# Wider warm-up products, earlier residual loads and one more raw weight tile in a single-core encoder layer

## The chip, the cores and the metric

The kernel runs on one core of a Trainium2 chip. The metric is the time in device microseconds of one execution. Each core has a matrix engine (TensorE, PE in the profile; its weight loads are PEld), a vector engine (VectorE, DVE), a scalar engine (ScalarE, ACT), a general engine (GpSimd, POOL) and a queue engine (SyncE, SP). DMAs are issued by SP, by POOL and, at the very end, by ACT.

## The reference

One layer of an encoder for 512 prompt tokens and 64 later tokens, in float32, with a model width of 1024, and a final norm:

```
x = x + Mixer(RMSNorm(x))          # gated DeltaNet branch and GLA branch, gated merge, then w_o
x = x + CrossAttn(RMSNorm(x), mem) # 4 heads into 256 memory tokens (w_mk, w_mv, w_mq, w_mo)
x = x + ConvFFN(RMSNorm(x))        # w_up, causal conv of width 3, SiLU gate, w_down
y = RMSNorm(x)
```

The recurrent states, the convolution tails and the memory keys and values are outputs too. The residual x has to be added back three times: after w_o, after w_mo and after w_down.

## The kernel before, in words

Activations lie feature-major: x is eight tiles of 128 features by 576 tokens (`x[0]` to `x[7]`). A weight tile is 128 partitions by 1024 columns, 512 KB. Every product is made in three passes of a reduced-precision float32 type: each operand is split into a high part and a low remainder, and high times high, low times high and high times low are summed in PSUM. For most weights the low part is not subtracted on an engine: ACT writes the negated high part, and a DMA that POOL issues adds the original weights onto it (`split_summed`, "accumulate" below). In the profile such a DMA is `w<-wt` or, where its source is a sum of weight blocks that lies in SBUF, `w<-ws`. The output projection w_o (`wo`), half of the gates, w_mo and most of the FFN use a scheme with seven block products per pair of tiles (`products`, named P1, Q5, Q6, P2, P3, Q7, Q4).

No scheduler of the framework orders the work. The kernel has its own planner, `Driver`: it goes through the program in PE's order, keeps a modelled clock `now`, estimates a start for every vector, scalar, POOL and DMA instruction from the costs in `FIXED` and `PACE`, and emits all of them in the order of these starts. Each engine then runs its own list in order and waits on semaphores. Small differences of modelled time can so swap neighbours in an engine's list, or move an operation that may run on DVE or on POOL (`X`) from one to the other.

Raw weights come by SP into the tiles `raw` (`RAWB` of them, in the pool `wp`, and after the mixer one more, `rawf`); in the profile that load is `wr<-wt`. A raw tile is free again when its split is done. Split weights lie in nine `w` tiles at that stage.

At the start PE multiplies a tile of ones with itself (`warm`, `NWARM` times) while the first x tiles and weights load and are split. Then come the q and k tiles of head 0 (`first2`, 16 groups of six products over 256 and 320 columns). Much later, `ATT` sets the order `mk 0, mv 0, mk 1, mk 2, wo, mv 1, mq 0, ...`: memory keys, the first memory values, more keys, the output projection w_o, and so on. Ahead of `wo` the eight residual tiles are loaded again from `xT` in pairs by `x_again`, since their first copies were given up: the pair 0 and 1 at the first memory values, and each next pair when w_o's product P1 for the pair before has been planned (`wo_finish`). The software descriptors of POOL's DMAs lie in a scratch at the foot of SBUF, with its default size.

Of the kernel before, what the change touches and what calls it, by code (L numbers as in the profile page):

```python
# [17 lines left out]
P = 128  # L18
# [7 lines left out]
SLOT = 584  # L26
HT = T // 2
NS = 56
RAWB = 3
WB = 6  # L30
WF = 3
RF = 1
# [2 lines left out]
HOP = 0.2  # L35
BACK = 6.0
MARGIN = 0.6
NWARM = 20


C_GMIX, C_GKV, C_GMEM, C_GFFN, C_GFIN = 0, 8, 16, 24, 32
# [417 lines left out]
def tile_trunk(ctx, tc, xT, memT, wt, wd, vec, cst, w0, wgate, st_gdn, st_conv, st_gla, st_ffn, ckT, cv,  # L459
               o_y, o_gdn_p, o_conv, o_gla_p, o_ffn, o_mk, o_mv, o_gdn_s, o_gla_s):  # L460
    nc = tc.nc
# [18 lines left out]
    def nm(s):  # L480
        cnt[0] += 1
        return f"{s}{cnt[0]}"
# [48 lines left out]
    def f(ap):  # L531
        return ap.bitcast(F32)
# [5 lines left out]
    def keep(t_):  # L538
        drv.pending.add(t_[:].tensor.name)
        return t_  # L540
# [5 lines left out]
    def raw_tile():  # L546
        if fp is not None and drv.first("rawf", RF, "raw", RAWB):
            return keep(drv.rotate("rawf", RF, fp.tile([P, 1024], F32, tag="rawf", name=nm("wr"), bufs=RF)))
        return keep(drv.rotate("raw", RAWB, wp.tile([P, 1024], F32, tag="raw", name=nm("wr"), bufs=RAWB)))

# [123 lines left out]
    ones_r = cp.tile([P, 128], F32R, name="onesr")  # L674
# [4 lines left out]
    G.memset(mhalf, -0.5)  # L679
    pw = pq.tile([P, 512], F32, tag="sm", name=nm("warm"))  # L680
    for _ in range(NWARM):
        PE.matmul(pw[:, 0:128], ones_r, ones_r, start=True, stop=True)


    vec_t = cp.tile([P, NV], F32, name="vec")
# [4 lines left out]
    x = []  # L690
    raws = [wp.tile([P, 1024], F32, tag="raw", name=nm("wr"), bufs=RAWB) for _ in range(2)]
    for t_ in raws:
        keep(drv.rotate("raw", RAWB, t_))

# [151 lines left out]
    def xs_of(hl, w=T):  # L846
        return [(a[:, 0:w], b[:, 0:w]) for a, b in hl]
# [697 lines left out]
    def products(pairs, ops, finish, late=None):  # L1545

        banks = {}
        for pair, prod in product_order(pairs, late is not None):
            if prod == "Q5" and late is not None:
                yield late  # L1550
                late = ()
            bank = pair, "b" if prod in ("Q5", "P3") else "c" if prod == "P2" else "a"
            start = bank not in banks
            if start:
                banks[bank] = sm()
            a, b, c = (banks[pair, i][:, 0:HT] if (pair, i) in banks else None for i in "abc")
            o = banks[bank][:, 0:HT]
            wh, wl = weight("*", (pair, prod), False)
            n = len(ops)
            for i, op in enumerate(ops):  # L1560
                h, lo = op[prod]
                PE.matmul(o, wh[:, 128 * i:128 * i + 128], h, start=start and i == 0, stop=False, skip_group_check=True)
                PE.matmul(o, wh[:, 128 * i:128 * i + 128], lo, start=False, stop=False, skip_group_check=True)
                yield 0.4
            for i, op in enumerate(ops):
                PE.matmul(o, wl[:, 128 * i:128 * i + 128], op[prod][0], start=False, stop=i == n - 1, skip_group_check=True)
            finish(pair, prod, a, b, c)
            drop(wh)
            fetch(wpos[0])
            yield 0.4  # L1570
# [8 lines left out]
    def xslot(i, s="x"):  # L1579

        return drv.rotate(f"F{i}", 1, fp.tile([P, SLOT], F32R if s != "x" else F32, tag=f"F{i}", name=nm(s), bufs=1))


    def main():
# [51 lines left out]
        for k in range(KT + 1):  # L1636
            for i, ps in enumerate(first2):
                j = k - i
# [164 lines left out]
        def x_again(m):  # L1803

            for i in (m, m + 1):
                x[i] = xslot(i)
                DMA(x[i][:, 0:T], xT[:, i, :])
# [6 lines left out]
        def wo_finish(pair, prod, a, b, c):  # L1814
            m = pair[0][1]
            xx, scale = (x[m], 0.5) if prod in ("P1", "Q6", "P3", "P2") else (x[m + 1], -0.5)
            half = N1 if prod in ("P1", "P2", "Q4") else N2
            V.scalar_tensor_tensor(xx[:, half], b if prod in ("Q5", "P3") else c if prod == "P2" else a, scale, xx[:, half],
                                   op0=ALU.mult, op1=ALU.add)
            if prod == "P1" and m < 6:  # L1820
                x_again(m + 2)
            if prod == ("P2" if m == 6 else "P3"):
                drv.spawn(c_norm(m, C_GMEM, acc, out))
            elif prod == "Q4":
                drv.spawn(c_norm(m + 1, C_GMEM, acc, out))

        def c_norm(m, gcol, acc_, out_):
            yield [x[m]]
            sq_acc(acc_, x[m], m == 0)
            drv.done.add(("sq", m))  # L1830
            if drv.ready(*(("sq", i) for i in range(8))):
                drv.spawn(c_rstat("n2", [(acc_, 0)], 4, True, 2.0))
            while not drv.ready("wo"):
                yield WAIT
            out_.append((m, norm_prep(x[m], vcol(gcol + m))))
            drv.done.add(("norm", gcol, m))

        for kd, i in ATT:
            if kd == "mk":
                yield from mem_keys(i)  # L1840
            elif kd == "mv":
                if i == 0:
                    x_again(0)
                yield from mem_values(i)
            elif kd == "wo":
                yield tuple(("wops", m) for m in range(1, 8, 2))
                yield from products(WPAIRS, [wops[m] for m in range(1, 8, 2)], wo_finish)
                drv.done.add("wo")
            else:
                if i == 0:  # L1850
                    yield tuple(("norm", C_GMEM, m) for m in range(8))
                    xs = xs_of([p for _, p in sorted(out, key=lambda t: t[0])])
                ckr, cvr = slot("ckr"), slot("cvr")
                DMA(r4(ckr[:, 0:512], 256), ckT[:, 2 * i:2 * i + 2, :])
                DMA(r4(cvr[:, 0:512], 256), cv[:, 256 * i:256 * i + 256].rearrange("(a p) d -> p a d", p=P))
                N["ks", i], N["vs", i] = split(ckr), cvr
                for m in (2 * i, 2 * i + 1):
                    b = []
                    yield from tile_proj("mq", m, xs, b)
                    if m == 0:  # L1860
                        yield ("n2",)
                        use_norm("n2")
                    q = slot("q")
                    evac(b[0], two(q))
                    h, lo = slot("qh", F32R), slot("ql", F32R)
                    A.copy(h[:, 0:T], q[:, 0:T])
                    X.tensor_tensor(lo[:, 0:T], q[:, 0:T], f(h[:, 0:T]), op=ALU.subtract)
                    N["q", m] = (h, lo)
                drv.spawn(c_att(i))
# [230 lines left out]
        for kd, i in FFN[:-1]:  # L2100
            if kd == "up":
                j = i
# [24 lines left out]
            elif kd == "dn1":  # L2127
                m, p = i
# [113 lines left out]
    def mem_keys(hd):  # L2242

        kr = slot("kraw")
        for j in range(2):
            wh, wl = weight("mk", 2 * hd + j)
            ps = big()
            for k in range(KT):
                a, b = N["mx"][k]
                mm3([(ps[:, 0, 0:256], slice(0, 256))], wh, wl, a, b, k, k == 0, k == 7)  # L2250
                if k % 2:
                    yield 0.7
            V.tensor_tensor(kr[:, 256 * j:256 * j + 256], ps[:, 0, 0:256], N["mbc"][:, 0:256], op=ALU.mult)
        DMO(o_mk[256 * hd:256 * hd + 256, :].rearrange("(j p) t -> p j t", p=P), r4(kr[:, 0:512], 256))
        N["k", hd] = split(kr)

    def mem_values(nh):

        vr = [slot("vraw") for _ in range(2)]
        ps = big()  # L2260
        for kp in range(4):
            wh, wl = weight("mv", nh * 4 + kp)
            for tt in range(2):
                c = slice(128 * tt, 128 * tt + 128)
                for k in range(2):
                    a, b = N["mx"][2 * kp + k]
                    w1, w2 = wh[:, 512 * k:512 * k + 512], wl[:, 512 * k:512 * k + 512]
                    PE.matmul(ps[:, tt, :], a[:, c], w1, start=(kp == 0 and k == 0), stop=False)
                    PE.matmul(ps[:, tt, :], a[:, c], w2, start=False, stop=False)
                    PE.matmul(ps[:, tt, :], b[:, c], w1, start=False, stop=(kp == 3 and k == 1))  # L2270
                    yield 1.0
        for tt in range(2):
            for j in range(2):
                A.activation(vr[j][:, 256 * tt:256 * tt + 256], ps[:, tt, 256 * j:256 * j + 256],
                             AF.Identity, scale=N["mrt"][:, tt:tt + 1])
        for j in range(2):
            hd = 2 * nh + j
            DMO(o_mv[:, 256 * hd:256 * hd + 256].rearrange("(a p) d -> p a d", p=P), r4(vr[j][:, 0:512], 256))
            N["v", hd] = split(vr[j])
# [153 lines left out]
```

## Time and profile before

| | |
|---|---|
| median of 3 runs | 1107.15 us (1104.71 to 1108.14) |
| the profiled execution | 1107.82 us, span 1106.1 us |
| PE busy | 1087.6 us (98% of the span) |
| DVE, ACT, POOL busy | 746.8, 700.5, 313.6 us |
| mean granted TensorE clock | 0.996 |
| DMA moved | 173.04 MB, mean 156 GB/s |
| DMAs that POOL issues | 209: 147 `w<-wt`, 33 `w<-wd` (w_down), 29 `w<-ws` |

Times inside the span are counted from its start. A row of the timeline has a start, a duration (from the start of the first to the end of the last where it is a group), the engine, the source line, the operation and its count; in brackets stands how long the engine had been idle, and what ended that. Nearly all rows say L257, the line of the planner's helper that records every operation, so they are told apart by tile names. Matmuls overlap in the rows, since each one's duration includes its way through the array; the distance between starts is the pace. PEclk in a table of windows is the clock granted to TensorE, 1.00 being full.

### The profile page before, as it was taken

How to read it: one execution, taken by the hardware profiler on the slowest of the kernel's cores; microseconds unless marked ns; L12 is line 12 of the kernel's file. 1: busy time of each engine (PE TensorE's matmuls, PEld its weight loads, DVE VectorE, ACT ScalarE, POOL GpSimd, SP SyncE). 2: the span in 40 equal slices, each digit the busy share in tenths (PEclk: the TensorE clock that was granted, in tenths of full speed). 3: DMA queues.
4: the chain of work that ended last, by engine and by line, in shares of the span. 5: the costliest groups of instructions: out<-in, count | busy, mean ns of one | idle time of the engine just before them, and what ended most of it. 6: DMA issues, size and time to landing. Idle time of an engine off the chain costs nothing. (4 is left out here: it accounts for less than half of the span.)

```text
span 1106.1 us, 21400 instructions
## 1 busy us (share of the span) xinstructions
PE 1087.6 (98%) x8215; PEld 1049.5 (95%) x8215; DVE 746.8 (68%) x1466; ACT 700.5 (63%) x1383; POOL 313.6 (28%) x539
## 2 busy tenths in 40 slices
PE   9999999999999999999999999999999999999997
PEld 8999989998988999998899999999999999999997
DVE  5566854864655866886746668768877777577766
ACT  6665645563755568465746658767776776668645
POOL 1243315230422232022110123334342333334222
PEclk9999999999999999999999999999999999999999
DMA  8666532453455778698792718766887888789754
GB/s 283 136 157 147 119 77 77 83 121 96 116 121 126 182 160 206 203 248 204 187 260 52 180 37 200 186 140 138 186 180 166 184 187 180 152 203 192 166 100 120
DMA packets 66886, 173.04 MB, mean 156 GB/s; under 512 B 7776, under 2 KB 14048, under 8 KB 66784
## 3 DMA queue, kind: packets, MB, share of 16 engines
q0 software_dynamic: 30096, 72.89, 38.4%
q1 hardware_dynamic: 36400, 98.26, 27.8%
q8 instruction: 65, 1.06, 0.4%
q10 hardware_dynamic: 288, 0.52, 0.1%
q14 instruction: 37, 0.30, 0.1%
HBM read 158.67 MB, written 5.37 MB: 148 GB/s over the span
## 5 line engine op out<-in xcount | busy, mean ns | idle before, releaser
L257 PE MATMUL big<-xh,w 128*128 128x256 f32 (+2 forms) x1568 | 293.0, 304 | 1.6 <-ACT xh L257 1.0
L257 POOL DMA_DIRECT2D w<-wt x147 | 131.0, 905 | 393.7 <-ACT w L257 265.7
L257 PEld LDWEIGHTS big<-xh,w 128*128 128x128 f32 x1568 | 235.9, 190 | 6.9 <-issue 2.0
L257 ACT CAST w<-wr 128x512 fp32r<-128x512 f32 (+3 forms) x201 | 158.6, 791 | 24.6 <-PE big L257 9.6
L257 PE MATMUL big<-xl,w 128*128 128x256 f32 (+2 forms) x784 | 168.4, 296 | 0.3 <-DVE xl L257 0.3
L257 ACT ACTIVATE w<-wr 128x512 fp32r<-128x512 f32 (+3 forms) x180 | 142.6, 793 | 38.1 <-PE sm L257 15.8
L257 PE MATMUL sm<-xh,w 128*128 128x290 f32 (+1 forms) x768 | 162.0, 298 | 0.6 <-ACT fu L257 0.5
L257 PE MATMUL sm<-ach,w 128*128 128x288 f32 (+2 forms) x624 | 128.8, 299 | 6.2 <-DMA w<-ws 2.6
L257 PEld LDWEIGHTS big<-xl,w 128*128 128x128 f32 x784 | 131.7, 189 | 0.7 <-DVE xl L257 0.7
L257 PEld LDWEIGHTS sm<-xh,w 128*128 128x128 f32 x768 | 126.3, 189 | 1.1 <-ACT fu L257 1.1
L257 PE MATMUL big<-ach,w 128*128 128x256 f32 x624 | 111.4, 295 | 0.5 <-ACT ach L257 0.5
L257 PEld LDWEIGHTS sm<-ach,w 128*128 128x128 f32 x624 | 102.0, 190 | 8.0 <-DMA w<-ws 3.1
L257 PE MATMUL sm<-xl,w 128*128 128x290 f32 (+1 forms) x384 | 103.1, 297 | 0.0
L257 PEld LDWEIGHTS big<-ach,w 128*128 128x128 f32 x624 | 94.6, 188 | 0.8 <-ACT ach L257 0.7
L257 ACT CAST w<-ws 128x512 fp32r<-128x512 f32 (+1 forms) x124 | 73.1, 602 | 31.1 <-DVE ws L257 15.3
L257 PE MATMUL sm<-acl,w 128*128 128x288 f32 (+2 forms) x312 | 84.7, 297 | 0.0
L257 DVE SCALAR_TENSOR_TENSOR fc<-fu,vec,fc 128x578 f32<-128x578 f32 x88 | 71.3, 828 | 7.6 <-ACT fc L257 7.2
L257 PEld LDWEIGHTS sm<-xl,w 128*128 128x128 f32 x384 | 71.8, 190 | 0.0
L257 DVE TENSOR_TENSOR w<-ws,w 128x512 fp32r<-128x512 f32 (+1 forms) x93 | 61.5, 673 | 14.3 <-ACT w L257 13.1
L257 PE MATMUL big<-acl,w 128*128 128x256 f32 (+1 forms) x312 | 66.7, 295 | 0.3 <-DVE acl L257 0.3
L257 PE MATMUL sm<-sh,w 128*128 128x290 f32 x288 | 61.5, 297 | 0.0
L257 PEld LDWEIGHTS sm<-acl,w 128*128 128x128 f32 x312 | 59.0, 191 | 0.0
(397 smaller groups left out, 2204.9 us busy)
## 6 DMA issues: line engine op xcount, KB each, us to landing
wr<-wt SPq DMA_DIRECT2D x134, 512.0 KB, 5.8
w<-wt POOLq DMA_DIRECT2D x60, 512.0 KB, 7.0
w<-wt POOLq DMA_DIRECT2D x87, 256.0 KB, 5.8
wr<-wd SPq DMA_DIRECT2D x24, 384.0 KB, 6.2
w<-wd POOLq DMA_DIRECT2D x24, 384.0 KB, 7.2
w<-ws POOLq DMA_DIRECT2D x29, 256.0 KB, 5.7
x<-xT SPq DMA_DIRECT2D x16, 288.0 KB, 5.8
mem<-memT SPq DMA_DIRECT2D x8, 256.0 KB, 4.4
```

The source lines that it names most:

```text
L257: fn(*args, **kw)
```

## The change

There are four edits in three ideas.

1. The warm-up has 11 products of 512 columns instead of 20 of 128: the same tile of ones is read four times by a broadcast.
2. All eight residual tiles are asked for at the first memory values, in one go; the three later calls from `wo_finish` are gone.
3. `RAWB` goes from 3 to 4, which costs 4 KB in each partition; the room is taken from the scratch of the dynamic DMAs, which is set to 8192 bytes.

```
-RAWB = 3
+RAWB = 4
-NWARM = 20
+NWARM = 11
 ...
-        PE.matmul(pw[:, 0:128], ones_r, ones_r, start=True, stop=True)
+        PE.matmul(pw, ones_r, ones_r.unsqueeze(1).broadcast_to([P, 4, 128]), start=True, stop=True)
 ...
             V.scalar_tensor_tensor(xx[:, half], b if prod in ("Q5", "P3") else c if prod == "P2" else a, scale, xx[:, half],
                                    op0=ALU.mult, op1=ALU.add)
-            if prod == "P1" and m < 6:
-                x_again(m + 2)
 ...
                 if i == 0:
-                    x_again(0)
+                    for j in range(0, 8, 2):
+                        x_again(j)
                 yield from mem_values(i)
 ...
-    nc = _bacc.Bacc("TRN2", target_bir_lowering=False, num_devices=1)
+    nc = _bacc.Bacc("TRN2", target_bir_lowering=False, num_devices=1, dynamic_dma_scratch_size=8192)
```

What this does to the lists of the engines. PE, ACT, DVE and POOL keep their order, apart from the warm-up, until the memory keys. In SP's list, before, at the first memory values (`wr` is a raw weight tile, `x` a residual tile, `o_mk` the store of a key):

```order
L257 DMA wr_5730<-wt 128x1024
L257 DMA x_5766<-xT 128x576
L257 DMA x_5767<-xT 128x576
L257 DMA wr_5771<-wt 128x1024
L257 DMA wr_5815<-wt 128x1024
L257 DMA wr_5848<-wt 128x1024
L257 DMA o_mk<-kraw_5697 128x2x256
```

And after, at the same place:

```order
L257 DMA wr_5721<-wt 128x1024
L257 DMA x_5757<-xT 128x576
L257 DMA x_5758<-xT 128x576
L257 DMA x_5759<-xT 128x576
L257 DMA x_5760<-xT 128x576
L257 DMA x_5761<-xT 128x576
L257 DMA x_5762<-xT 128x576
L257 DMA x_5763<-xT 128x576
L257 DMA x_5764<-xT 128x576
L257 DMA wr_5768<-wt 128x1024
L257 DMA wr_5816<-wt 128x1024
L257 DMA o_mk<-kraw_5688 128x2x256
```

Six more residual tiles stand between two raw weight tiles, and one raw tile fewer stands ahead of the key's store.

SP's list, before, where w_o begins:

```order
L257 DMA o_mk<-kraw_5959 128x2x256
L257 DMA x_6061<-xT 128x576
L257 DMA x_6062<-xT 128x576
L257 DMA wr_6155<-wt 128x1024
L257 DMA wr_6156<-wt 128x1024
L257 DMA x_6198<-xT 128x576
L257 DMA x_6199<-xT 128x576
L257 DMA wr_6291<-wt 128x1024
L257 DMA wr_6292<-wt 128x1024
L257 DMA x_6330<-xT 128x576
L257 DMA x_6331<-xT 128x576
```

And after:

```order
L257 DMA o_mk<-kraw_5957 128x2x256
L257 DMA wr_6166<-wt 128x1024
L257 DMA wr_6167<-wt 128x1024
L257 DMA wr_6293<-wt 128x1024
L257 DMA wr_6294<-wt 128x1024
```

Only the raw weights of w_o are left there.

From the memory keys on, neighbours change places on ACT, DVE and POOL, and in the attention some groups of PE too. POOL's list, before, in the queries (`w<-wt` is an accumulate; `kvl`, `acl` are low parts of an operand):

```order
L257 DMA w_6894<-wt 128x1024
L257 TENSOR_TENSOR kvl_7100<-ckr_7097,kvh_7099 128x512
L257 DMA w_7287<-wt 128x1024
L257 DMA w_7411<-wt 128x1024
L257 DMA w_7443<-wt 128x1024
L257 DMA w_7526<-wt 128x1024
```

And after:

```order
L257 DMA w_6886<-wt 128x1024
L257 TENSOR_TENSOR acl_7219<-ao_7190,ach_7218 128x576
L257 DMA w_7249<-wt 128x1024
L257 DMA w_7381<-wt 128x1024
L257 TENSOR_TENSOR acl_7444<-ao_7419,ach_7443 128x576
L257 DMA w_7477<-wt 128x1024
L257 DMA w_7509<-wt 128x1024
```

One low part goes from POOL to DVE, and two others, for the attention's output `ao`, come from DVE to POOL, each ahead of an accumulate.

## The prediction

> **What bounds the kernel now.** I read the page first: how busy the engines are.
>
> ```profile
> span 1106.1 us, 21400 instructions
> PE 1087.6 (98%) x8215; PEld 1049.5 (95%) x8215; DVE 746.8 (68%) x1466; ACT 700.5 (63%) x1383; POOL 313.6 (28%) x539
> q0 software_dynamic: 30096, 72.89, 38.4%
> ```
>
> PE is busy for all but 18.5 us of the span, and the change takes no product away but the warm-up's. So it can win only PE's idle time, or time in which PE is busy but slow. The profiled execution took 1107.82 us, 1.7 more than its span and 0.67 more than the median of 1107.15; sums below are made against it. Next I read the table of waits, for PE; the columns are microseconds in total, times, the longest.
>
> ```profile
> PE sm L257 <- DMA w<-ws: 2.6, 2, 2.4
> PE sm L257 <- DVE x L257: 1.8, 4, 0.7
> PE sm L257 <- DMA w<-wt: 1.6, 1, 1.6
> ...
> ```
>
> The largest wait is for a DMA, an accumulate of w_o. Then I looked for slow time in windows of 1 us around it; the first number is the length, then PE, PEld, DVE, ACT and POOL busy, the granted clock, the DMA share and GB/s.
>
> ```profile
> 502.00:503.00 1.00, 1.00 (x8) 1.00 (x7) 0.46 (x1) 0.00 (x0) 0.00 (x0) 0.70 1.04 358
> 503.00:504.00 1.00, 1.00 (x6) 1.00 (x5) 0.00 (x0) 0.00 (x0) 0.00 (x0) 0.50 1.10 234
> 504.00:505.00 1.00, 1.00 (x6) 1.00 (x6) 0.51 (x2) 0.46 (x1) 0.00 (x0) 0.50 1.07 315
> 505.00:506.00 1.00, 1.00 (x6) 1.00 (x6) 0.97 (x2) 1.00 (x3) 0.53 (x1) 0.60 1.11 266
> ```
>
> After the wait the granted clock falls to one half for about 3.4 us. The missing parts add up to 0.30 + 0.50 + 0.50 + 0.40 = 1.7 us, which no table of idle time shows. PE has another slow stretch at the start; its timeline shows it by the pace.
>
> ```profile
> 1.00 4.34 PEld L257 LDWEIGHTS warm<-onesr 128*128 128x128 f32 x20 [1.00 <-POOL onesr L257]
> 1.00 4.53 PE L257 MATMUL warm<-onesr 128*128 128x128 f32 x20 [1.00 <-POOL onesr L257]
> 6.05 1.10 PE L257 MATMUL big<-xh,w 128*128 128x256 f32 x2 [0.52 <-ACT w L257]
> 7.24 0.63 PE L257 MATMUL big<-xl,w 128*128 128x320 f32 x1
> 7.67 1.16 PE L257 MATMUL big<-xh,w 128*128 128x256 f32 x4
> 9.11 1.16 PE L257 MATMUL big<-xh,w 128*128 128x256 f32 x4
> 10.55 0.84 PE L257 MATMUL big<-xh,w 128*128 128x256 f32 x4
> 11.50 0.69 PE L257 MATMUL big<-xh,w 128*128 128x256 f32 x4
> 12.29 0.69 PE L257 MATMUL big<-xh,w 128*128 128x256 f32 x4
> ```
>
> The same six products take 1.44 us from 7.67 to 9.11 and 0.79 from 11.50 to 12.29. The full pace begins about 10.7, some 3.4 us after the products became dense at 7.24. I read both places alike: the clock is judged over stretches of about 3.4 us, goes up after a dense one and down after a thin one.
>
> **Warm-up.** Six products of 1728 columns in 1.44 us are 1.2 columns a nanosecond. A warm-up product of 128 columns is then 0.107 us of streaming, but one comes every 4.53 / 20 = 0.227 us, at the pace of its weight load (4.34 / 20 = 0.217). So the array streams 47% of the time, and the clock does not rise. A product of 512 columns streams 0.427 us, longer than the load of the next weights: the array is full. Eleven take 4.7 us; after the first load they end at about 5.9, ahead of 6.05, when the first real product is released by the split of its weights, so the warm-up itself delays nothing.
>
> Dense from 1.2 on, PE should have the full clock between 4.6 and 8. If it is there by 7.3, the 3.4 us up to 10.7 that ran at half pace shrink by 1.7. The most is half of 6.05 to 10.7, 2.3; the least is nothing, since a fast warm-up ends early, and the idle time up to 6.05 and the first waits for splits make a thin stretch, after which the clock may fall again. A loss past 0.1 is excluded, since 5.9 lies ahead of 6.05 even at half pace. I take 1.7, for the phase in which this trace's clock rose. What could take the 1.7 back is the next weights, but they are split well ahead:
>
> ```profile
> 18.30 1.03 ACT L257 CAST w<-wr 128x1024 fp32r<-128x1024 f32 x1
> 23.45 0.53 PE L257 MATMUL big<-xh,w 128*128 128x256 f32 x2
> ```
>
> The high part is there at 19.33, and PE would begin at 21.75 instead of 23.45. Up to the memory keys no engine's order changes.
>
> The Trainium skill, page "TensorE: Matmul & The Clock Gate", section "Part 1: The HAM clock gate", says that warming up costs about 3.4 us of time and not a number of products, and that what is issued later runs at the full rate. By that the old warm-up of 4.53 us would do, and this term would be 0; the row at 7.67, still at half pace, speaks against it here.
>
> **Residual tiles.** The wait at 501.21 is for the low part of w_o's second Q5. Its accumulate and what SP issued around it:
>
> ```profile
> 501.21 0.93 PE L257 MATMUL sm<-ach,w 128*128 128x288 f32 x5 [2.38 <-DMA w<-ws]
> 487.09 0.86 POOL L257 DMA_DIRECT2D w<-wt  x1 [1.96 <-ACT w L257]
> 489.18 0.86 POOL L257 DMA_DIRECT2D w<-wt  x1 [1.22 <-ACT w L257]
> 490.98 0.87 POOL L257 DMA_DIRECT2D w<-ws  x1 [0.94 <-ACT w L257]
> 487.15 1.08 SPq L257 DMA_DIRECT2D x<-xT  x2
> 488.33 0.93 SPq L257 DMA_DIRECT2D wr<-wt  x2
> 489.36 1.05 SPq L257 DMA_DIRECT2D x<-xT  x2
> 490.00:500.00 10.00, 8.83 (x67) 8.60 (x65) 6.31 (x13) 5.04 (x9) 1.77 (x3) 1.00 1.06 290
> w<-ws POOLq DMA_DIRECT2D x29, 256.0 KB, 5.7
> ```
>
> It was issued at 490.98 and landed at about 501.2, 10.2 us later, where the median of such a DMA is 5.7. The DMA engines were full, at 290 GB/s. Four residual tiles of 128 by 576 floats, 1.15 MB, went out in the 3.3 us before it: 4.0 us of DMA time. Without them it lands about 497 and PE's demand stands at 498.8, so the wait ends: 2.6 us with the small one of the same row of waits (0.23, at 489), and the 1.7 us of half clock behind it. I keep 0.3 as a rest, since raw weights move up into the room. Ends: 0 gained, if POOL's own DMAs were the queue, and 4.3.
>
> Now the place to which six tiles move: 1.73 MB, 6.0 us at 290 GB/s, in SP's queue ahead of the raw weights of the last memory values and the keys. Who waits is ACT, which splits them, and PE behind it.
>
> ```profile
> 449.45 0.91 SPq L257 DMA_DIRECT2D x<-xT  x2
> 451.13 9.79 SPq L257 DMA_DIRECT2D wr<-wt  x3
> 460.71 1.06 ACT L257 CAST w<-wr 128x1024 fp32r<-128x1024 f32 x1 [1.91 <-PE big L257]
> 471.83 0.62 PE L257 MATMUL big<-w,mh 128*128 128x512 f32 x2
> ```
>
> The raw tile issued at 451.13 is the one split at 460.71, and that split waits for PE to free a `w` tile, not for the DMA. It would go out at about 453, when eight issues of 0.46 are through, and land about 458 to 459. The margin is about 2 us for the split, and PE multiplies by that tile, the fourth of the first values, only from 471.83. I take 0; only a landing past 469 would cost, since the split's two halves take some 2.3 us.
>
> **Raw tile and scratch.** The split at 460.71 waited for PE to free a `w` tile and not for its raw tile; where that is so, one more raw tile brings loads forward but no products. I take 0; at best it ends the 1.6 us wait for `w<-wt`, at worst it crowds an accumulate by 512 KB, 1.8 us at 290 GB/s. The scratch holds descriptors. 30096 packets for POOL's 209 DMAs are 144 each, 9 on each of 16 engines. Their issues take 0.905 to 0.914 us on the mean (third number), with no wait for room:
>
> ```profile
> L257 POOL DMA_DIRECT2D w<-wt x147 | 131.0, 905 | 393.7 <-ACT w L257 265.7 <-DVE kvl L257 38.1 <-ACT yc L257 19.4
> L257 POOL DMA_DIRECT2D w<-ws x29 | 26.5, 914 | 41.4 <-ACT w L257 36.2 <-PE sm L257 4.6 <-issue 0.6
> ```
>
> I take 0 for half the room.
>
> **Reordering.** From the keys on neighbours swap. The nearest price is POOL against DVE for a low part: 1.43 against 0.75 us.
>
> ```profile
> 654.63 1.43 POOL L257 TENSOR_TENSOR acl<-tw,ach 128x576 fp32r<-128x576 f32 x1 [22.31 <-ACT ach L257]
> 653.75 0.75 DVE L257 TENSOR_TENSOR acl<-tu,ach 128x576 fp32r<-128x576 f32 x1
> ```
>
> Two such come to POOL ahead of accumulates for the queries: 0.7 us each, hidden behind PE if the accumulates have slack. A luckier order could also end the wait of 1.8 us for `x` in the table. Ends: -1.8 and +4.1, one more stall like that at 501; I take +0.4, beside the hidden end, since POOL's queue only gets longer.
>
> The sum: 1107.82 - 1.7 - 4.3 + 0.3 + 0.4 = 1102.5, which is 0.42% under the median. A measurement of this kernel can tell about 0.3%, 3.3 us, from no change: faster is below 1103.8, slower above 1110.5.
>
> **The rivals.** *The warm-up gains nothing*: the clock still rises about 10.7, by the skill's rule or because it falls again. For it speaks the idle gap before 6.05; against it the 47%. 1104.2.
>
> *The burst was not the cause*: the accumulate waited in POOL's own queue, behind two accumulates issued at 487 and 489. Then 2.4 + 1.7 stay: 1102.5 - 0.3 + 4.3 = 1106.5. Against it: the DMA engines were full, and SP's 2.2 MB were most of it.
>
> *Slower: accumulates for the queries come late.* POOL's second `acl` waits for ACT's `ach`, and an accumulate stands behind it. If that makes it land over 2 us after PE wants it, PE idles and the clock falls, as at 501: 2.4 + 1.7 = 4.1 each. It decides from about 2 us, since a wait of 1.6 us left the clock at 1.00:
>
> ```profile
> 670.07 0.93 PE L257 MATMUL sm<-ach,w 128*128 128x288 f32 x5 [1.62 <-DMA w<-wt]
> 671.00:672.00 1.00, 1.00 (x9) 1.00 (x9) 0.95 (x2) 1.00 (x3) 0.18 (x1) 1.00 0.70 131
> ```
>
> Two such give 1102.5 + 8.2 = 1110.7. For it: two of POOL's operations were moved. Against: PE's three waits for accumulates (2 and 1 in the table) lie at 489, 501 and 670, none in the queries.
>
> *Slower: the smaller scratch is full.* It decides when more packets are in flight than fit. With 5.7 us to land and an issue every 2 us (487, 489, 491), some 3 DMAs, 27 packets an engine, are in flight. If POOL had to wait for one landing, 5.7 us, at each of the 29 `w<-ws`, that is 165 us: 1268. By the skill's pages "SBUF — State Buffer", section "SBUF size: 192, 224, or 256?" (the scratch is that ring), and "DMA: Bandwidth & Descriptors", section "Terms" (16 bytes each), 8192 bytes hold 512 by my estimate; no run here shows that.
>
> **How the numbers follow.** Forecast 0.55, of which 0.52 below 1103.8; no gain at the start 0.15 (0.03 below the line, 0.12 within); burst not the cause 0.14 (within); late accumulates 0.12 (0.10 slower, 0.02 within); scratch 0.04 (slower). Faster 0.55, same 0.31, slower 0.14. The range runs from 1099.5, where 2.3 is gained at the start, no 0.3 is left at w_o and 1.8 is gained instead of 0.4 lost, to 1107.5, which holds the first three cases; the last two, 0.16, are left out.
>
> **What would show it.** Right: six products about 0.79 us apart from before 8 us on, the first real product still near 6.05; no wait for `w<-ws` over 0.5 in w_o and no granted clock of 0.5 there; eight `x` issues near 449 and no PE wait for memory weights. Wrong: half pace at 9, a wait for `w<-ws` near 497, or new DMA waits of over 2 us in the queries or the FFN with half a clock behind them.

## The result, and the profile after

The changed kernel takes 1103.51 us, the median of 12 runs (1101.77 to 1105.99), against 1107.15 us before (12 runs, 1104.71 to 1108.87). The ratio is 0.997, with a 95% interval of 0.996 to 0.998. The forecast was 1102.5 us, and "faster" the likeliest case; that was right, though by a hair: the gain is 3.64 us, and the line lay at 3.3. As the experiments show, the two gains were forecast about rightly, and one edit that was put at nothing, the fourth raw tile, costs 1 to 3 us. That the time came within 1.0 us of the forecast is in part luck: the sum started from an execution about 1 us slower than usual, which hid part of that cost.

The profiled execution took 1103.10 us. Its page:

```profile
span 1101.2 us, 21348 instructions
PE 1084.6 (98%) x8206; PEld 1045.5 (95%) x8206; DVE 745.0 (68%) x1464; ACT 702.8 (64%) x1383; POOL 313.5 (28%) x541
q0 software_dynamic: 30096, 72.89, 38.7%
```

The span is 4.9 us shorter; idle time of PE went from 18.5 to 16.6 us, and busy time by 3.0, though the products are the same but for the warm-up's: the rest is pace. PE's waits (total, times, longest):

```profile
PE sm L257 <- DVE x L257: 2.4, 3, 1.3
...
PE sm L257 <- DMA w<-ws: 1.0, 2, 0.6
...
PE sm L257 <- DMA w<-wt: 0.9, 1, 0.9
PE sm L257 <- ACT qh L257: 0.8, 1, 0.8
```

The wait for `w<-ws` fell from 2.6 to 1.0, that for `w<-wt` from 1.6 to 0.9; the one for `x` rose from 1.8 to 2.4, and one of 0.8 for `qh` is new. PE's timeline at the start, and the row that stood at 23.45 before:

```profile
1.00 5.06 PE L257 MATMUL warm<-onesr 128*128 128x512 f32 x11 [1.00 <-POOL onesr L257]
6.16 0.88 PE L257 MATMUL big<-xh,w 128*128 128x256 f32 x2
7.35 0.42 PE L257 MATMUL big<-xl,w 128*128 128x320 f32 x1 [0.20 <-DVE xl L257]
7.61 0.68 PE L257 MATMUL big<-xh,w 128*128 128x256 f32 x4
8.52 0.69 PE L257 MATMUL big<-xh,w 128*128 128x256 f32 x4
9.31 0.69 PE L257 MATMUL big<-xh,w 128*128 128x256 f32 x4
...
22.05 0.53 PE L257 MATMUL big<-xh,w 128*128 128x256 f32 x2
```

From 8.52 six products take 0.79 us, where they took 1.44 before at 7.67. PE is 1.40 us ahead at 22.05 and stays so: its first wait for `kgt` stands at 199.91 instead of 201.31. The trace also records the granted clock directly, from its first rise on (ahead of that rise a window reads 1.00, though the pace is half). The rise stands at 10.88 us before and at 6.48 after. Now w_o: the residual loads and raw weights (SP), the accumulate (POOL, and its time to land), PE's two waits, and the clock (third number from the right).

```profile
434.12 16.35 SPq L257 DMA_DIRECT2D x<-xT  x8
486.03 1.61 SPq L257 DMA_DIRECT2D wr<-wt  x3
490.17 0.86 POOL L257 DMA_DIRECT2D w<-ws  x1 [1.19 <-ACT w L257]
w<-ws POOLq DMA_DIRECT2D x1, 256.0 KB, 8.5
488.76 0.37 PE L257 MATMUL sm<-ach,w 128*128 128x288 f32 x1 [0.49 <-DVE x L257]
498.67 0.94 PE L257 MATMUL sm<-ach,w 128*128 128x288 f32 x5 [0.64 <-DMA w<-ws]
498.00:500.00 2.00, 1.36 (x11) 1.33 (x11) 0.48 (x2) 1.24 (x3) 1.71 (x2) 1.00 1.19 274
500.00:502.00 2.00, 2.00 (x18) 2.00 (x17) 1.46 (x3) 1.26 (x3) 0.00 (x0) 1.00 0.94 278
```

The accumulate lands after 8.5 us instead of 10.2, PE waits 0.64 instead of 2.38, and the clock stays at 1.00. But the DMA engines are as full as before (282 GB/s from 490 to 500, against 290): SP now issues three raw tiles at 486 to 488 instead of two. Behind w_o (the first row, the first product after it, stood at 536.67 before, and the last row at 1097.77):

```profile
531.06 0.62 PE L257 MATMUL big<-w,mh 128*128 128x512 f32 x2
627.72 0.39 PE L257 MATMUL sm<-kvh,qh 128*128 128x256 f32 x1 [0.79 <-ACT qh L257]
664.72 0.93 PE L257 MATMUL sm<-ach,w 128*128 128x288 f32 x5 [0.93 <-DMA w<-wt]
1079.01 0.37 PE L257 MATMUL sm<-ach,w 128*128 128x288 f32 x1 [1.33 <-DVE x L257]
1092.96 1.91 PE L257 MATMUL sm<-keep,gx 128*128 128x128 f32 x16
```

Where the 4.81 us of PE's end came from, by the same rows in both traces: 1.40 by 200 us, 5.61 at the first product behind w_o, 4.69 by the attention's last operand (652.23 before, 647.54 after), 5.18 in the FFN (754.73, 749.55), and some given back at 1079. So w_o gave 4.2 us, and 0.9 was lost again in the attention, most of it in the new wait for `qh`. The stretch at half clock at the start of the FFN, near 700 before, is there after as well (0.66 on the mean from 695 to 700).

### The profile page after: what moved, and what is told of

Read it like the earlier page. It is cut to its first block, busy times and chain, and to the rows that moved or that the text cites. A ratio compares the mean times of both kernels' runs of the same rounds, so it can differ in the third digit from the quotient of the medians.

```text
span 1101.2 us, 21348 instructions
## 1 busy us (share of the span) xinstructions
PE 1084.6 (98%) x8206; PEld 1045.5 (95%) x8206; DVE 745.0 (68%) x1464; ACT 702.8 (64%) x1383; POOL 313.5 (28%) x541
## 3 DMA queue, kind: packets, MB, share of 16 engines
q8 instruction: 65, 1.06, 0.4%
## 5 line engine op out<-in xcount | busy, mean ns | idle before, releaser
L257 POOL DMA_DIRECT2D w<-wt x147 | 133.6, 915 | 372.6 <-ACT w L257 314.5
```

Of the source, the lines that this page charges most:

```text
L257: fn(*args, **kw)
```

## The experiments

Medians of all kernels that were timed more than once, each with its ratio to the kernel before on the same chip. Two further kernels have one execution each, the narrow warm-up (1103.27) and the burst of four (1103.31); they are read by their traces alone.

| kernel | us | ratio, 95% interval |
|---|---|---|
| warm-up alone | 1103.77 | 0.9971 (0.996 to 0.9982) |
| residual tiles alone | 1103.43 | 0.9971 (0.9959 to 0.9982) |
| fourth raw tile and scratch alone | 1106.99 | 1.0005 (0.9993 to 1.0018) |
| warm-up and residual tiles, three raw tiles | 1101.63 | 0.996 (0.9947 to 0.9973) |
| the same, other chip | 1102.10 | 0.9955 (0.994 to 0.9971) |
| the changed kernel once more | 1104.14 | 0.9979 (0.9968 to 0.999) |
| three raw tiles, burst of loads that nobody reads | 1102.87 | 0.9971 (0.9959 to 0.9983) |
| three raw tiles, filling products | 1101.14 | 0.9949 (0.9935 to 0.9963) |
| the same, other chip | 1101.04 | 0.9946 (0.9932 to 0.9961) |
| the same with 14 warm-up products | 1101.06 | 0.9944 (0.9928 to 0.9959) |

### The parts alone

Each is the kernel before with one edit of the change, or with two.

```
-NWARM = 20                    # warm-up alone
+NWARM = 11                    # and the product of 512 columns
```

> The kernel before with the wider warm-up alone. Theory: the clock is full some 3 us earlier, so PE's list is 1.4 us ahead from 23 us on (as in the changed kernel's trace) and nothing else moves: 1105.7 against 1107.15, a ratio of 0.9987; the wait for the w_o accumulate at about 499.8 stays near 2.4 us with a half clock behind it. Rival: a DMA that is not PE-bound stands behind (the raw weights come at the pace of the DMAs), so the 1.4 us turn into a longer wait somewhere before 500 us: 1107.1.

```
-            if prod == "P1" and m < 6:      # residual tiles alone
-                x_again(m + 2)
 ...
-                    x_again(0)
+                    for j in range(0, 8, 2):
+                        x_again(j)
```

> The kernel before with all residual tiles loaded at the first memory values, raw tiles and scratch as before. Theory (the burst of residual tiles made the accumulate of w_o's second Q5 late): the wait for w<-ws near 501 falls from 2.38 to under 0.7, no granted clock of 0.5 near 502; 3.5 us less: 1103.7. Rival (the accumulate is late in POOL's own queue, or the raw weights fill the room at once): the wait stays over 2 us, 1106.5 to 1107.2. Second rival: the gain needs the fourth raw tile, since x now stands ahead of raw tiles in SP's queue; then a new wait of 1 to 2 us for w<-wt shows between 450 and 480 us.

```
-RAWB = 3                      # raw tile alone, with dynamic_dma_scratch_size=8192
+RAWB = 4
```

> The kernel before with a fourth raw tile out of a scratch of 8192 bytes, nothing else. Theory: 0, within 1 us of 1107.15, the w_o wait stays over 2 us. Rival (the raw tile is what made w_o faster: raw weights are there earlier and are out of the accumulate's way): the wait at 501 falls below 1 us and 3 us are gained: 1104. Rival (the smaller scratch holds POOL up): POOL's mean issue of an accumulate rises above 0.91 us and the time above 1108.

The fourth kernel has the first two edits and three raw tiles.

> The changed kernel without its fourth raw tile and with the default scratch. Theory: the gains of the warm-up and of the residual tiles add and the raw tile gives nothing: 1107.15 - 1.4 - 3.5 = 1102.3, within 1.2 of the changed kernel's 1103.5. Rival (the raw tile carries part of it): 1105 to 1106.5, slower than the changed kernel by 2 or more, with a wait for w<-ws of over 1.5 us in w_o.

The residual tiles alone gain 3.7 us, near the 3.5 expected. The accumulate lands in 6.7 us, no wait stands near 501 and no stretch at half clock behind it; a wait of 0.96 at 490, for the accumulate before it, is left:

```profile
490.00 0.94 PE L257 MATMUL sm<-ach,w 128*128 128x288 f32 x5 [0.96 <-DMA w<-ws]
w<-ws POOLq DMA_DIRECT2D x1, 256.0 KB, 6.7
```

The raw tile alone gives nothing. The two gains together give 5.5 us (5.3 on the other chip): 1.9 under the changed kernel, where a difference of at most 1.2 was expected. So the fourth raw tile seems to cost something in the full change.

The warm-up alone gained 3.4 us, more than the 1.4 expected. In its trace PE is 1.5 us ahead after the first tiles, the wait for the accumulate is 1.95 instead of 2.38, and this time the clock does not fall behind it:

```profile
498.58 0.94 PE L257 MATMUL sm<-ach,w 128*128 128x288 f32 x5 [1.95 <-DMA w<-ws]
500.00:502.00 2.00, 2.00 (x17) 2.00 (x16) 0.98 (x2) 0.93 (x2) 0.01 (x1) 1.00 1.07 310
```

With the raw tile alone the wait is 2.26 and the clock stays up too. So a wait of about 2 us costs the further 1.7 us in some executions and not in others; on what that hangs is taken up in "How the clock rises". Whether the warm-up makes it rarer at w_o, or six runs were lucky, these runs don't separate. That either edit alone can save the same 1.7 us is the likely reason why the gains of the parts add up to more than they give together.

### The fourth raw tile

> The changed kernel once more, beside the next two on the same chip. Theory: the fourth raw tile costs about 1.5 to 2 us, since it reorders DVE near the end (a sum of squares ahead of the last residual adds: the wait for x at 1079 is 1.33 us against 0.20 without it) and leaves 0.5 and 0.6 us of waits in w_o: 1103.5, and 2 us above the kernel without it (1101.6). Rival: the 1101.63 of that kernel was the luck of its chip and runs: 1102 to 1103 here, level with it.

The time fits the theory, 1104.14; the kernel without the raw tile was not run on that chip. All 24 runs of the changed kernel have a median of 1103.83, the 18 with three raw tiles 1101.95; they did not run side by side, but each stands against the kernel before on its own chip, and there the difference is 0.0010 to 0.0024, or 1.1 to 2.7 us. The raw tile and the smaller scratch were always changed together, except that the two burst kernels below have the small scratch with three raw tiles. Two mechanisms are in the traces. The first is at w_o. SP and the accumulate's time to land with three raw tiles, in the run on the second chip:

```profile
486.96 0.45 SPq L257 DMA_DIRECT2D wr<-wt  x1
488.25 0.35 SPq L257 DMA_DIRECT2D wr<-wt  x1
w<-ws POOLq DMA_DIRECT2D x1, 256.0 KB, 6.9
```

One raw tile fewer stands ahead of the accumulate, and it lands after 6.9 us instead of 8.5 (8.1 in the changed kernel's second trace), in time for PE. The second is near the end. There DVE in the changed kernel makes two sums of squares ahead of the residual adds that free PE's `sm` buffers:

```profile
1076.88 1.61 DVE L257 TENSOR_TENSOR acc<-acc,sq 128x576 f32<-128x576 f32 x2
1078.41 1.01 DVE L257 TENSOR_TENSOR x<-x,sm 128x288 f32<-128x288 f32 x2
```

In the first trace with three raw tiles one of the sums stands on POOL, and PE's wait is 0.20 instead of 1.33:

```profile
1082.20 1.44 POOL L257 TENSOR_TENSOR acc<-acc,sq 128x576 f32<-128x576 f32 x1
1081.52 0.37 PE L257 MATMUL sm<-ach,w 128*128 128x288 f32 x1 [0.20 <-DVE x L257]
```

The same wait is 1.32 to 1.39 in all three traces with four raw tiles, and 0.19 to 0.21 in all eleven with three, the two with the small scratch among them; so it is the raw tile that reorders this place. Between the changed kernel's second trace and the one from the second chip, neither with a stretch at half clock, PE takes 1.7 us longer from the end of the first tiles to its last group (20.01 to 1091.98 against 20.75 to 1091.03): it loses 0.8 us in w_o, 0.4 near 665 and 1.1 at 1078, and wins 0.6 elsewhere.

### Is it the bytes ahead of the accumulate?

The six transfers are brought back as loads that nobody reads, with three raw tiles and the smaller scratch.

```
+        dump = cp.tile([P, 2 * T], F32, name="dump")
 ...
+            if prod == "P1" and m < 6:
+                for i in range(2):
+                    DMA(dump[:, i * T:i * T + T], xT[:, m + 2 + i, :])
```

> The changed kernel without its fourth raw tile, scratch 8192, and in w_o, where the three later pairs of residual tiles were loaded before, two loads of 128x576 each into a tile that nobody reads: the six transfers are back, and nobody waits for them. Theory (the bytes of the burst made the accumulate late): the wait for w<-ws near 499 is back at 1.9 to 2.4 us, 2 to 4 us slower than 1101.6: 1103.6 to 1105.6. Rival (it was the order of the planner, or POOL's own queue): no such wait, 1101.6. If neither the burst nor the scratch matters, the same 1101.6.

```
+            if prod == "P1" and m == 0:      # dump of 4 * T, one burst
+                for i in range(4):
+                    DMA(dump[:, i * T:i * T + T], xT[:, 2 + i, :])
```

> As the burst before, but with all four transfers of 128x576 in one go at w_o's first product, ahead of the accumulate of the second Q5 (1.18 MB, 4.1 us at 290 GB/s), three raw tiles. In the runs so far that accumulate took 6.4 to 7.2 us to land with nothing in its way, 8.1 to 8.5 with the fourth raw tile or with one pair ahead of it, 9.2 to 10.2 with two pairs. Theory (bytes ahead of it in the queue of the DMA engines): 10 us or more, and a wait of PE for w<-ws of 2 us or more near 499. Rival (the lateness hangs on the planner's order, not on the bytes): 7 to 8.5 us, a wait under 1 us.

Neither wait came out as large as expected: 0.72 and 1.19 us, where 1.9 to 2.4 and 2 or more were forecast, and the first kernel is 1.2 to 1.8 us slower by its ratio, not 2 to 4. The time to land did follow the bytes, in one trace of each. In the first the second pair went out at 490.96, behind the accumulate of 490.01, so only one pair stood ahead of it.

```profile
499.19 0.93 PE L257 MATMUL sm<-ach,w 128*128 128x288 f32 x5 [1.19 <-DMA w<-ws]
w<-ws POOLq DMA_DIRECT2D x1, 256.0 KB, 9.0
```

What SP had issued in the 4 to 5 us ahead of that accumulate, over all traces:

| loads ahead of it | MB | to land, us | PE waited, us |
|---|---|---|---|
| 2 raw tiles (residual tiles moved, three raw tiles; seven traces) | 1.05 | 6.4 to 7.2 in five; 7.9; 8.5 | none; none; 0.45 |
| 3 raw tiles (changed kernel; two traces) | 1.57 | 8.1, 8.5 | 0.24, 0.64 |
| 2 raw tiles and one pair (burst) | 1.64 | 8.5 | 0.72 |
| 2 raw tiles and two pairs (burst of four) | 2.23 | 9.0 | 1.19 |
| the same (warm-up alone; before) | 2.23 | 9.2; 10.2 | 1.95; 2.38 |
| the same and a raw tile just ahead (raw tile alone) | 2.75 | 9.5 | 2.26 |

PE comes to the tile 7.2 to 8.1 us after the issue (498.83 less 490.98 before, 498.03 less 490.17 after), and what the landing takes beyond that is the wait. So the bytes ahead make the accumulate late, whether they are residual tiles, raw weights or of no use; but equal amounts differ by up to 2.1 us from trace to trace, and that stays unexplained. The table is of this one accumulate: in six of the seven traces of its first row PE still waits 0.49 to 0.96 us for the accumulate before it, near 489, and 1.06 in the changed kernel's second trace.

### How the clock rises

```
-NWARM = 20          # with the residual tiles moved
+NWARM = 34          # still 128 columns
```

> Residual tiles moved, three raw tiles, and a warm-up of 34 products of the old 128 columns, 7.7 us instead of 4.5. Theory (what counts is the share of time in which the array streams; 47% is too little): the clock is still at half pace when the real products begin near 8.7 us and rises 3.4 to 6.8 us after that, so groups of six products come 1.44 us apart until 12 or later. Rival (3.4 us of any products in a row raise it): groups of six are 0.79 us apart from the first.

```profile
1.00 7.52 PE L257 MATMUL warm<-onesr 128*128 128x128 f32 x34 [1.00 <-POOL onesr L257]
8.31 0.79 PE L257 MATMUL big<-xh,w 128*128 128x256 f32 x2
9.38 1.09 PE L257 MATMUL big<-xh,w 128*128 128x256 f32 x4
10.57 0.69 PE L257 MATMUL big<-xh,w 128*128 128x256 f32 x4
11.37 0.69 PE L257 MATMUL big<-xh,w 128*128 128x256 f32 x4
```

After 7.5 us of narrow products in a row the first real products still run at half pace, so the rival falls. But the full pace is there by 10.57, earlier than the 12 us that theory gave: about 2 us of dense products on top of narrow ones were enough. The recorded clock rises at 10.26 us here, and at 10.26 to 11.31 in all four traces with narrow products; in the ten with wide ones it rises at 4.39 to 6.73. By the Trainium skill, page "TensorE: Matmul & The Clock Gate", section "Part 1: The HAM clock gate", a warm-up is a matter of about 3.4 us of time and not of a number of products; this run disagrees where they stream only 47% of it. The same section of the Trainium skill says that the window runs free of the kernel's start, and there the traces agree: the clock rose at 6.48 us in one execution of the changed kernel and at 4.86 in the other.

The records also show when a wait is followed by half clock. From its first rise on, in every trace, the clock changes only at whole multiples of 3.413 us: in the trace of before it stays full for 144 of them, then half for 1, full for 57, half for 1, full for 117. So each execution can be cut into stretches of 3.413 us. Of the 2.38 us of wait before, 2.23 lie in one stretch (498.98 to 502.39), and the clock falls at its end. The 1.95 of the warm-up alone is split into 1.62 and 0.33 at 498.25, the 2.26 of the raw tile alone into 0.96 and 1.30 at 499.42, and neither is followed by a fall. Over all 14 traces, PE waits over 1.5 us ten times behind the first tiles: the two waits with 2.23 and 2.29 us in one stretch are followed by half clock, the eight with at most 1.74 are not. What counted, as far as these ten go, is how much of a wait falls into one stretch, and where the stretches begin differs from one execution to the next. No run moved the stretches on purpose.

A fall right behind the first rise is in the profiled execution of the kernel with three raw tiles, at 1108.20 us its slowest. PE at full pace overtook the splits, waited, and the clock fell again:

```profile
8.84 0.60 PE L257 MATMUL big<-xl,w 128*128 128x256 f32 x2 [0.32 <-DVE xl L257]
10.00:11.00 1.00, 1.00 (x6) 1.00 (x6) 1.00 (x3) 0.88 (x3) 0.00 (x0) 0.50 1.05 403
```

Its first tiles ended 0.8 us later than before the change (the products `sm<-x,w` begin at 22.21 against 21.38). In the eight other traces with 11 wide products they begin 0.6 to 1.6 us earlier.

### Filling the wait at the start of the FFN

Both traces lose 1.7 us near 700, where PE waits 0.97 us for `xh` and then makes ten products of one column. In the trace after:

```profile
693.17 0.54 PE L257 MATMUL big<-xh,w 128*128 128x290 f32 x2 [0.97 <-ACT xh L257]
694.34 1.16 PE L257 MATMUL sm<-keep,acc 128*128 128x1 f32 x10
```

The filling keeps three raw tiles.

```
                     h, lo, _ = fx[k]
+                    if k == 7:
+                        idle = sm()
+                        for _ in range(4):
+                            PE.matmul(idle, ones_r, ones_r.unsqueeze(1).broadcast_to([P, 4, 128]), start=True, stop=True)
```

> The changed kernel without its fourth raw tile, and with four warm-up products of 512 columns ahead of the product that waits 0.97 us for xh at the start of the FFN (about 697 us). They take 0.85 us of a wait of 0.97. Theory (a stretch with half of its time unstreamed drops the clock; most executions lose 1.7 us there): the granted clock is 1.00 from 695 to 705 and the runs lie at 0.999: 1.0 to 1.5 us less than 1101.6. Rival (the stretch still counts as thin, because of the ten products of one column behind it): the same 1101.6. Rival (the fillers come too late or delay the xh product): 0.2 to 0.5 us more.

> The changed kernel without its fourth raw tile, once more, beside the next two on one chip. Theory: 1101.6 as before, some 2 us under the changed kernel. Rival: 1103, level with it.

> Three raw tiles, four filling products at the start of the FFN, and 14 warm-up products instead of 11. Theory (a warm-up that lasts until the splits of the first tiles are there leaves no thin stretch between 6 and 9 us, so that the clock doesn't fall again): the slowest executions go, the median is 0.3 to 0.8 us below the same with 11. Rival (three more products at half pace end at 7.3 and delay the first real one by up to 1.2 us, and the splits would not have fed PE faster): 0.3 to 1.0 us above.

> Three raw tiles and the four filling products, with 11 warm-up products, beside the two above. Theory: 0.5 to 1.2 us under the same kernel without the filling products, since the executions with a clock of 0.997 and less (6 of 12 without them) go. Rival: no difference.

The first filled trace, and the other one at the same place:

```profile
691.43 1.09 PE L257 MATMUL sm<-onesr 128*128 128x512 f32 x4
695.00:697.00 2.00, 2.00 (x16) 1.97 (x17) 1.73 (x6) 2.00 (x3) 1.03 (x2) 1.00 0.04 16
```

```profile
690.84 1.09 PE L257 MATMUL sm<-onesr 128*128 128x512 f32 x4
697.00:699.00 2.00, 2.00 (x10) 2.00 (x10) 1.73 (x6) 2.00 (x4) 2.00 (x6) 0.50 0.80 221
```

The filling does not end the fall, and probably makes it rarer. On one chip the filled kernel has 1101.04 and the unfilled 1102.10, with intervals that overlap; over all chips 12 filled runs lie between 1100.41 and 1102.39, 18 unfilled between 1100.33 and 1108.20. The mean clock of a run suggests why. In the trace with four such stretches it is 0.993, with two 0.996, with one 0.997 (0.998 once), with none 0.998 or 0.999. It was 0.997 or less in 48 of 58 runs of the kernel before, in 17 of 24 of the changed one, in 9 of 18 with three raw tiles and in none of the 18 filled ones (the one filled trace with a stretch has 0.998, so that some may hide there). Three more warm-up products change nothing (1101.06 against 1101.04), where 0.3 to 0.8 us was expected. The filled kernels are the fastest, about 0.5% under the one before.

## Why the prediction was right, and what it missed

**Warm-up, -1.7.** The mechanism held, and 1.40 was measured in the trace. The clock rose even sooner than the 7.3 taken, at 6.48, and 4.4 us of half pace less would be worth 2.2. But the first product came 0.11 us later (the warm-up ended at 6.06, not 5.9), and PE at full pace ran up against the splits: a wait of 0.20, and 0.91 us for the six products from 7.61. The rival "it falls again" is real, but in one trace of nine. One reading was loose: PE had been dense from 6.05 on, not from 7.24, and counted back by 3.413 us, the stretch that ended with the rise at 10.88 began at 7.46.

**Residual tiles, -4.3 with 0.3 left.** The cause was named rightly, as the landing times show on the whole. The waits for accumulates in w_o fell from 2.6 to 0.64 and the half clock went; behind w_o PE had gained 4.2 us past the start, where 4.0 were forecast: 2.0 from these waits, 1.7 from the clock, and the rest from waits for `x`: 0.37 and 0.69 went, 0.49 came. What was left is over the 0.3 taken and over the 0.5 named as a sign: 0.64, and 1.06 and 0.24 in the second trace. The step that was off took the 1.7 us of half clock as certain. It comes in some executions: waits of 1.95 and 2.26 left the clock alone, as they fell into two stretches. The forecast also started from a profiled execution with two stretches at half clock, 1.0 us above the median of the 58 runs of before made beside the experiments (1106.78). Two sums are slightly off: four residual tiles are 1.18 MB and six 1.77, not 1.15 and 1.73, and the lower end of the range adds up to 1099.4.

**Room at the memory values, 0, and scratch, 0.** Right. The `x` loads went out from 434 to 450, earlier than thought, and PE waited for no memory weight. POOL's issues did not slow:

```profile
L257 POOL DMA_DIRECT2D w<-wt x147 | 133.6, 915 | 372.6 <-ACT w L257 314.5 <-ACT yc L257 19.4 <-DMA wr<-wt 7.6
L257 POOL DMA_DIRECT2D w<-ws x29 | 25.4, 876 | 51.8 <-ACT w L257 47.7 <-PE sm L257 3.4 <-issue 0.7
```

**Raw tile 0, reordering +0.4.** The raw tile is the term that was mis-sized: it costs 1.1 to 2.7 us (1.9 between the pooled medians). The prediction had the mechanism as its worst end ("it crowds an accumulate by 512 KB, 1.8 us") and took 0, from the one split that did not wait for its raw tile. It judged the edit at the memory values, whereas the edit acts wherever SP can run ahead, above all in the room just made at w_o. The reordering that cost most, 1.1 us at 1079, lies on DVE near the end, where the prediction did not look. The other, the wait of 0.79 for `qh`, comes with the residual tiles: it stands in ten of the eleven traces that move them, and in none of the three that don't.

**The rivals.** *The burst was not the cause* is refuted by the residual tiles alone, which take the wait at 501 away, and by the landing times. *Late accumulates for the queries* did not come: the one new wait there is for ACT's `qh`. *The smaller scratch is full* did not come.

The forecast of 1102.5 so fits the kernel without the fourth raw tile (1101.63 and 1102.10) better than the one it was made for.

## What to carry to other kernels

A late accumulate is priced first by the bytes that other queues have issued in the few microseconds ahead of it; when these are taken out, look at what moves up into the room, since one more prefetch buffer can fill it again. Give a stall of about 2 us two prices, with and without the half clock behind it, and a chance for each; one trace shows only one of them. Where the pace of products and the table of the clock disagree, as at the start here, trust the pace. A short wait in front of products that hardly stream is a place for filling products, if they are shorter than the wait.

## What the runs showed that was not expected

The clock's fall is not tied to a place in the program: executions showed between none and four stretches at half clock, which seems to account for much of their scatter (1100.33 to 1108.20 us in 18 runs). The length of a wait alone does not decide it: 2.26 us, split over two stretches of 3.413, passed unpunished, while 1.2 us of waits with ten one-column products behind them cost about 1.7 us in five of the eleven traces without filling.
